# Last block of a three-block model: the scan's memory pool in two parts, the first chunk's decays and scores beside the convolution's norm

## The chip, the cores and the metric

One NeuronCore of a Trainium2 chip runs the whole program. The metric is the device time of one execution in microseconds (us); the time of a kernel is the median of its runs.

## What is computed

Three residual blocks run in series on 1024 tokens of width 1024, all in float32. The last one, which the change is mostly about, is this (cut):

```python
h = layer_norm(x, ln_emb_g, ln_emb_b)
proj = einsum('bld,de->ble', h, w_in)
xs, z, bm, cm, dt_raw, glu, cgate = split(proj, SPLITS, axis=-1)
xbc = silu(causal_depthwise_conv(concat([xs, bm, cm]), ssm_conv_w) + ssm_conv_b)
y = ssd_chunked(xh, dt, a, bm_c, cm_c) + d_skip * xh      # a scan over 8 chunks of 128 tokens, 2 groups
y_ssm = rms_norm_by_group(y * silu(z)) * ssm_norm_g
u = glu_a * sigmoid(glu_b)
u = causal_depthwise_conv(u, conf_conv_w) + conf_conv_b   # 31 taps
y_conf = silu(layer_norm(u, conf_ln_g, conf_ln_b)) * silu(cgate)
out = concat([y_ssm, y_conf]) @ w_out + b_out
h = layer_norm(alpha * h + out); h = layer_norm(alpha * h + sigmoid(h @ w_gate) * (p @ w_proj))
```

In a chunk the scan's output is `(C B^T * exp(segment sums)) @ xdt`, the diagonal part, plus `C @ state * exp(cumulative sum)`, the part that comes from the chunks before; the state is then decayed and raised by `B^T @ (xdt * decay)`. The second block, where the other part of the change lies, is an attention that keeps the top k keys of each query (called DSA here) and ends with a product with `od_w_out`.

## The kernel before

Each float32 product is made of three matmuls of 128x512 on split operands (lines 148 to 150, a "step" below): a weight is loaded as `wraw` on SP's queue, copied by ACT (`w`, L122), and its rest is taken by POOL (`w`, L123). `wraw` has 3 buffers, `w` has 13.

**Last block (`phase_c`).** DVE makes the 31-tap convolution channel by channel (`cy`, `cc`, L1323) and adds the channels up in `acc` (L1326). Meanwhile PE works through a list of filling steps: `filling` yields 128 steps for `cgate`, 128 for `z` and then 128 for the second half of `w_out`, on tiles `msC` that are made of the gated convolution output `cc`. PE's order in this place is written out by hand: `take(n)` issues the next n filling steps, `next(norm)` one part of `conf_norm`, and each turn of the loop over `ssd` one part of the scan. `conf_norm` makes the mean `mu` (PE, L1538), takes it off `cc` (DVE, L1544), squares (ACT) and sums (POOL), makes the variance `var` (PE, L1554), the factor `rb` (PE, L1560), multiplies (DVE, L1566) and ends with a silu on ACT (L1567). After that POOL multiplies `cc` by the gate `cgl` (L1395, 16 pieces, at most 4 for each turn of the scan), and only then can ACT and POOL make `msC` (L1358, L1359).

A chunk of `ssd` loads `xh`, `bct` and, for each of two groups, `ld`; DVE adds (L1698) and ACT takes Exp (L1700), which gives the decays; PE makes the scores `cb` (L1703, L1704); DVE multiplies (`cb` L1706, `ld` L1711); POOL makes `xd`, `xe` and scales `xh` (L1716 to L1723); for each group PE then makes `yoff`, `ydiag` and `inc`, and DVE and POOL add up `yS` and the state `st`. The tile sets of the scan lie in the pool `ssd`, which is opened after the pool `c_u` (the convolution's `acc`, `u` and the norm's `rsc`) is closed, and takes its memory. ACT, DVE, POOL and SP run their queues in order; a scheduler sets the order from the program, with PE's order given.

**Second block (`phase_b`).** POOL and ACT norm the query tiles (`hm`, `hr`, `qo`, then a store `d_q` from POOL's queue) while DVE finishes the top k. Then `DSA.front` loads a bias for each head as `lgB` on SP's queue and makes the softmax, unit by unit, and `out_tile` multiplies finished tiles by `od_w_out`. The first 8 weights of it are loaded only behind the bias loads of the second unit (`front_first`).

Of the kernel before, what the change touches and what calls it, by code (L numbers as in the profile page):

```python
# [11 lines left out]
F32 = mybir.dt.float32  # L12
# [7 lines left out]
P = 128  # L20
# [828 lines left out]
def phase_b(k, x, hout, hB):  # L849
# [64 lines left out]
    for b in range(2, 8):  # L914
        n = (b + 1) * P
# [78 lines left out]
    mix = mp.tile([P, 8, L], F32, name="mixB")  # L994
    with ExitStack() as c2:
        dp = c2.enter_context(k.pool("b_dsa"))
        wo = []
        ds = DSA(k, ep, dp, d_q, d_T, d_gate, kT, vB, sc, kg, mix)
        units = [(b, kv) for b in DORD for kv in range(2)]
        front = ds.front  # L1000

        def front_first(b, kv):
            front(b, kv)
            if (b, kv) == units[1]:
                with tc.issue_after(ds.bias_load.ins):
                    wo.extend(k.wchunk(Wo, 0, 512))
        ds.front = front_first
        pipeline(ds, units, lambda b: out_tile(k, mo, gp, b, 0, [mix], wo, x, hout, "sq", 1))
    sR.close()
    k.wdve = WDVE[3]  # L1010
# [149 lines left out]
class DSA:  # L1160
# [22 lines left out]
    def front(self, b, kv):  # L1183

        k, p, kT = self.k, self.p, self.kT
        with k.tc.high_priority(offset=2 * WPRIO if b == DORD[0] else 0):
            qT = self.load(b, kv)
        nc = k.nc
        V, S, G = nc.vector, nc.scalar, nc.gpsimd
        n = (b + 1) * P  # L1190
        st = p.tile([P, 5, 4], F32, tag="st", name="stB", bufs=3)
        hs, ts_ = slice(kv * 4, kv * 4 + 4), slice(b * P, (b + 1) * P)
        lgs = []
        for i in range(4):
            h = kv * 4 + i
            lg = (self.pe if i < 2 else p).tile([P, L], F32, tag="lg", name="lgB", bufs=4)
            lgs.append(lg)
            with k.tc.high_priority(offset=WPRIO):
                self.bias_load = nc.sync.dma_start(lg[:, :n], dap(self.d_T, h * P * 1152 + 127 + P * (7 - b), [[1151, P], [1, n]]))
            if b >= 2:  # L1200
                G.tensor_tensor(lg[:, :n], lg[:, :n], self.masks[b], op=ALU.add)  # L1201
            mx = -3e38
            for j, c0 in enumerate(range(0, n, 512)):
                w = min(512, n - c0)
                ps = k.ps("s")
                k.mm3(ps[:, :w], qT[:, 0, i], qT[:, 1, i], kT[:, 0, kv, c0:c0 + w], kT[:, 1, kv, c0:c0 + w],
                      True, True)
                V.tensor_tensor_reduce(lg[:, c0:c0 + w], ps[:, :w], lg[:, c0:c0 + w], 1.0, mx, ALU.add, ALU.max,
                                       st[:, 3 + j, i:i + 1])
                mx = st[:, 3 + j, i:i + 1]  # L1210
            V.tensor_scalar(st[:, 0, i:i + 1], mx, -1.0, None, op0=ALU.mult)
            S.activation(lg[:, :n], lg[:, :n], AF.Exp, bias=st[:, 0, i:i + 1], accum_out=st[:, 1, i:i + 1])
            V.reciprocal(st[:, 2, i:i + 1], st[:, 1, i:i + 1])
            S.activation(lg[:, :n], lg[:, :n], AF.Copy, scale=st[:, 2, i:i + 1])
        self.lgs[b, kv] = lgs
# [57 lines left out]
def phase_c(k, out, hC):  # L1273
# [18 lines left out]

    sF, (rp,) = stack(k.pool("c_conf"))
    cc = rp.tile([P, 8, L], F32, name="cc")
    sV, (up,) = stack(k.pool("c_u"))
    acc = up.tile([P, L], F32, name="acc")
    for j in range(4):
        w = [k.wpiece(W, kk, [(2576 + j * 256, 256), (3600 + j * 256, 256)]) for kk in range(KT)]
# [81 lines left out]
    with tc.manual_schedule(engines={mybir.EngineType.PE}):  # L1380
        take(128 + 58)
        norm = conf_norm(k, up, cc, acc, cw)
        for n in (43, 8, 0):
            next(norm)
            take(n)
        next(norm, None)
        sV.close()
        sS, (sp,) = stack(k.pool("ssd"))
        gated = 0
        for i, _ in enumerate(ssd(k, sp, steps, dtt, dtx, d_xs, d_bc, d_ys, d_cs)):  # L1390
            for _ in range(min(4, 16 - gated)):
                ct, cs = gated % 8, slice(gated // 8 * 512, gated // 8 * 512 + 512)
                cg = stage("cgl")
                nc.sync.dma_start(cg, d_cg[ct * P:(ct + 1) * P, cs])
                G.tensor_tensor(cc[:, ct, cs], cc[:, ct, cs], cg, op=ALU.mult)  # L1395
                gated += 1
            take(0 if i == 0 else 4 if i < 5 else 0 if i < 7 else 3)
        take(500)
    held.close()
    sS.close()  # L1400
# [265 lines left out]
    return tri, nacs, eac, dst, cdc  # L1666


def ssd(k, p, steps, dtt, dtx, d_xs, d_bc, d_ys, d_cs):
    nc, ins = k.nc, k.ins  # L1670
    V, S, G, T = nc.vector, nc.scalar, nc.gpsimd, nc.tensor
    f = lambda a: a.rearrange("p a b -> p (a b)")
    tri, nacs, eac, dst, cdc = steps
    first = {t: [p.tile([P, 512], F32, tag=t, name=n, bufs=2) for _ in range(2)]
             for t, n in (("y", "yS"), ("xe", "xe"), ("xd", "xd"))}

    def half(tag, name):
        return first[tag].pop(0) if first[tag] else p.tile([P, 512], F32, tag=tag, name=name, bufs=2)
    st = [p.tile([P, 512], F32, name=f"st{g}") for g in range(2)]
    for g in range(2):  # L1680
        V.memset(st[g], 0.0)
    b64 = lambda a, g, c: a[:, c, g * 8:g * 8 + 8].unsqueeze(2).to_broadcast([P, 8, 64])
    b64a = lambda a, c: a[:, c].unsqueeze(2).to_broadcast([P, 16, 64])
    h3 = lambda a: a.rearrange("p (h d) -> p h d", d=64)
    for c in range(8):
        ts_ = slice(c * P, (c + 1) * P)
        xhs = []
        for g in range(2):
            xhs.append(p.tile([P, 512], F32, tag="xh", name="xh", bufs=3))
            nc.sync.dma_start(xhs[g], d_xs[ts_, g * 512:(g + 1) * 512])  # L1690
        bct = p.tile([P, 4, P], F32, tag="bct", name="bct", bufs=2)
        nc.sync.dma_start(bct, d_bc[:, ts_].rearrange("(a n) t -> n a t", a=4))
        lds = []
        for g in range(2):
            ld = p.tile([P, 8, P], F32, tag="ld", name="ld", bufs=3)
            lds.append(ld)
            nc.sync.dma_start(ld, dap(d_cs, (c * 16 + g * 8) * P, [[0, P], [1, 8 * P]]))
            V._custom_dve(TENSOR_ADD_SAT, out=ld, in0=ld,  # L1698
                          in1=nacs[:, c, g * 8:g * 8 + 8].unsqueeze(2).to_broadcast([P, 8, P]), s0=0.0, s1=-3e38)
            S.activation(ld, ld, AF.Exp)  # L1700
        ps = k.ps("sd", "cb")
        for g in range(2):
            T.matmul(ps[:, g * P:(g + 1) * P], bct[:, g], bct[:, 2 + g], start=True, stop=True)  # L1703
            T.transpose(ps[:, 256 + g * P:256 + (g + 1) * P], bct[:, g], k.ident)  # L1704
        cb = p.tile([P, 2, P], F32, tag="cb", name="cb", bufs=1)
        V.tensor_tensor(cb, ps[:, :256].rearrange("p (g l) -> p g l", g=2),  # L1706
                        tri.unsqueeze(1).to_broadcast([P, 2, P]), op=ALU.mult)
        bt = p.tile([P, 2, P], F32, tag="bt", name="bt", bufs=1)
        S.activation(f(bt), ps[:, 256:512], AF.Copy)
        for g in range(2):  # L1710
            V.tensor_tensor(lds[g], lds[g], cb[:, g].unsqueeze(1).to_broadcast([P, 8, P]), op=ALU.mult)  # L1711
        yield
        xds, xes = [], []
        for g in range(2):
            xd = half("xd", "xd")
            G.tensor_tensor(h3(xd), h3(xhs[g]), b64(dtt, g, c), op=ALU.mult)  # L1716
            xds.append(xd)
        for g in range(2 if c < 7 else 0):
            xe = half("xe", "xe")
            G.tensor_tensor(h3(xe), h3(xds[g]), b64(dst, g, c), op=ALU.mult)  # L1720
            xes.append(xe)
        for g in range(2):
            G.tensor_tensor(h3(xhs[g]), h3(xhs[g]), dtx[:, 2, g * 8:g * 8 + 8].unsqueeze(2).to_broadcast([P, 8, 64]),  # L1723
                            op=ALU.mult)
        for g in range(2):
            gs = slice(g * 512, g * 512 + 512)
            po = k.ps("sd", "yoff")
            T.matmul(po, bct[:, 2 + g], st[g], start=True, stop=True)
            y = half("y", "yS")
            V.tensor_tensor(h3(y), h3(po), b64(eac, g, c), op=ALU.mult)  # L1730
            yield
            pd = k.ps("sd", "ydiag")
            for h in range(8):
                T.matmul(pd[:, h * 64:(h + 1) * 64], lds[g][:, h], xds[g][:, h * 64:(h + 1) * 64],  # L1734
                         start=True, stop=True)
            V.tensor_tensor(y, pd, y, op=ALU.add)
            G.tensor_tensor(y, y, xhs[g], op=ALU.add)
            nc.sync.dma_start(d_ys[ts_, gs], y)
            if c < 7:
                pi = k.ps("sd", "inc")  # L1740
                T.matmul(pi, bt[:, g], xes[g], start=True, stop=True)
                V.tensor_tensor(h3(st[g]), h3(st[g]), b64(cdc, g, c), op=ALU.mult)
                V.tensor_tensor(st[g], pi, st[g], op=ALU.add)
            yield
# [34 lines left out]
```

## Time and profile before

| | |
|---|---|
| median of 3 runs | 2072.5 us (2067.56, 2072.5, 2074.84) |
| the profiled execution's own time | 2079.29 us |
| its span, first to last instruction | 2077.6 us |
| TensorE (PE) busy | 1939.3 us, 93% |
| VectorE (DVE), ScalarE (ACT), GpSimd (POOL) busy | 1408.7, 922.2, 946.9 us |
| mean granted TensorE clock | 0.965 |

The profiled execution stands 6.8 us above the median of the runs. A timeline row gives start and length of a group of like instructions on one engine, and in brackets how long the engine stood idle before it and what released it. A row of the windows gives the busy time of each engine in a stretch.

### The profile page before, as it was taken

The page shows a single profiled execution, that of the slowest core. Times are in us where ns is not written, and L with a number is a line of the kernel's source. Part 1 is how long each engine was busy: PE and PEld are TensorE (multiplying, and loading weights), DVE is VectorE, ACT ScalarE, POOL GpSimd, SP SyncE. Part 2 cuts the span into 40 slices and gives each one's busy share as a digit, 9 for nine tenths or more (in the row PEclk, how much of TensorE's full clock was granted, in tenths as well). Part 3 has the DMA queues.
Part 4 walks back from the last instruction along what each step waited for, and adds up shares of the span by engine and source line. Part 5 has one row for each costly group of instructions (what it writes and reads, how often), then busy time and mean ns, then how long its engine had stood idle before and what let it go on. Part 6 is the DMA issues. An engine that isn't in the chain of part 4 may idle for free.

```text
span 2077.6 us, 27679 instructions
## 1 busy us (share of the span) xinstructions
PE 1939.3 (93%) x9291; PEld 1569.5 (76%) x9291; DVE 1408.7 (68%) x2847; ACT 922.2 (44%) x1831; POOL 946.9 (46%) x812
## 2 busy tenths in 40 slices
PE   7988989998999999799989999999999789999998
PEld 6767767777888877678767788788888657778786
DVE  8475513674559997677655399999998456657737
ACT  5222326664555897677756211245323431143210
POOL 5576415545422146765557221222223797545304
PEclk9998989999999999899999999999999889999999
DMA  6543342312322211563445232223333465474542
GB/s 202 152 123 101 109 147 84 112 44 92 99 64 77 67 42 57 176 215 136 132 160 182 88 101 68 71 93 92 112 105 109 147 207 187 142 253 157 178 147 102
DMA packets 166825, 256.20 MB, mean 123 GB/s; under 512 B 29207, under 2 KB 77677, under 8 KB 166683
## 3 DMA queue, kind: packets, MB, share of 16 engines
q1 hardware_dynamic: 155178, 232.43, 35.1%
q10 hardware_dynamic: 10224, 17.82, 2.3%
q0 software_dynamic: 1280, 4.20, 0.5%
q8 instruction: 73, 1.20, 0.2%
q14 instruction: 70, 0.57, 0.1%
HBM read 185.35 MB, written 75.06 MB: 125 GB/s over the span
## 4 chain that ended last, share of the span: by engine, by line
PE 59%; DVE 15%; DMA 9%; issue 6%; ACT 5%; POOL 5%; SPq 1%; DVEq 0%; POOLq 0%; ACTq 0%
PE mm L150 11%; PE mm L148 11%; PE mm L149 11%; DVE tkj L1114 2%; PE ydiag L1734 1%; PE pb L148 1%; PE pb L150 1%; PE pg L148 1%; PE pg L150 1%; PE pb L149 1%; PE pg L149 1%; PE pa L149 1%; PE pa L150 1%; PE pa L148 1%; POOL w L123 1%
## 5 line engine op out<-in xcount | busy, mean ns | idle before, releaser
L123 POOL TENSOR_TENSOR w<-wraw,w 128x512 fp32r<-128x512 f32 (+1 forms) x238 | 326.3, 1385 | 653.8 <-ACT w L122 647.2
L1323 DVE SCALAR_TENSOR_TENSOR cy<-u,cw,cy 128x1024 f32<-128x1024 f32 x232 | 298.6, 1287 | 5.7
L122 ACT ACTIVATE w<-wraw 128x512 fp32r<-128x512 f32 (+1 forms) x238 | 145.9, 623 | 186.2 <-DMA wraw<-in_w_in_dram 47.2
L148 PE MATMUL mm<-hnTC,w 128*128 128x512 f32 (+1 forms) x336 | 131.7, 392 | 0.0
L150 PE MATMUL mm<-hnTC,w 128*128 128x512 f32 (+1 forms) x336 | 131.6, 392 | 0.0
L149 PE MATMUL mm<-hnTC,w 128*128 128x512 f32 (+1 forms) x336 | 131.5, 391 | 0.0
L148 PE MATMUL mm<-w,ms 128*128 128x512 f32 x256 | 106.0, 414 | 9.0 <-ACT ms L1055 7.9
L1201 POOL TENSOR_TENSOR lgB<-lgB,sc 128x1024 f32<-128x1024 f32 (+5 forms) x48 | 81.1, 1724 | 67.1 <-DMA lgB<-d_T 65.5
L150 PE MATMUL mm<-w,ms 128*128 128x512 f32 x256 | 105.4, 413 | 4.5 <-POOL ms L1056 3.7
L1112 ACT ACTIVATE tkj<-sc,tks 128x896 bf16<-128x896 f32 (+2 forms) x93 | 96.7, 1041 | 22.1 <-DVE tks L1108 19.4
L149 PE MATMUL mm<-w,ms 128*128 128x512 f32 x256 | 104.0, 406 | 1.6 <-POOL w L123 1.6
L148 PE MATMUL mm<-w,hnTA 128*128 128x512 f32 (+1 forms) x192 | 72.6, 381 | 8.7 <-DVE qo L429 7.8
L148 PE MATMUL mm<-hnTB,w 128*128 128x512 f32 (+2 forms) x208 | 78.4, 377 | 0.2 <-DVE wit L886 0.2
L148 PE MATMUL mm<-w,hnTB 128*128 128x512 f32 x192 | 75.7, 395 | 2.9 <-ACT w L122 2.6
L149 PE MATMUL mm<-hnTB,w 128*128 128x512 f32 (+2 forms) x208 | 78.1, 376 | 0.0
L150 PE MATMUL mm<-hnTB,w 128*128 128x512 f32 (+2 forms) x208 | 78.1, 375 | 0.0
L149 PE MATMUL mm<-w,hnTB 128*128 128x512 f32 x192 | 74.7, 391 | 0.9 <-POOL w L123 0.9
L150 PE MATMUL mm<-w,hnTB 128*128 128x512 f32 x192 | 74.9, 390 | 0.0
L150 PE MATMUL mm<-w,hnTA 128*128 128x512 f32 (+1 forms) x192 | 72.8, 380 | 0.0
L149 PE MATMUL mm<-w,hnTA 128*128 128x512 f32 (+1 forms) x192 | 72.4, 378 | 0.3 <-POOL w L123 0.3
L148 PEld LDWEIGHTS mm<-hnTC,w 128*128 128x128 f32 (+1 forms) x336 | 61.6, 183 | 14.5
L149 PEld LDWEIGHTS mm<-hnTC,w 128*128 128x128 f32 (+1 forms) x336 | 61.6, 183 | 14.4
(612 smaller groups left out, 5896.0 us busy)
## 6 DMA issues: line engine op xcount, KB each, us to landing
wraw<-in_w_in_dram SPq DMA_DIRECT2D x56, 256.0 KB
wraw<-in_od_w_in_dram SPq DMA_DIRECT2D x48, 256.0 KB
wraw<-in_ev_w_in_dram SPq DMA_DIRECT2D x32, 256.0 KB
wraw<-in_w_in_dram SPq DMA_DIRECT2D x64, 128.0 KB
wraw<-in_w_out_dram SPq DMA_DIRECT2D x32, 256.0 KB
ld<-d_cs SPq DMA_DIRECT2D x16, 512.0 KB
hr<-h SPq DMA_DIRECT2D x24, 256.0 KB
d_T<-d_row SPq DMA_DIRECT2D x8, 576.0 KB
```

What stands on the lines that cost most here:

```text
L122: nc.scalar.activation(t[:, 0, :o], raw[:, :o], AF.Copy)
L123: nc.gpsimd.tensor_tensor(t[:, 1, :o], raw[:, :o], t[:, 0, :o].bitcast(F32), op=ALU.subtract)
L148: mm(out, aH, bH, start=start, stop=False)
L149: mm(out, aH, bL, start=False, stop=False)
L150: self.last = mm(out, aL, bH, start=False, stop=stop)
L1112: S.activation(self.junk(n), sc[b], AF.Sign, bias=cand[:, i:i + 1], accum_out=cnt[:, i:i + 1])
L1114: V.tensor_scalar(self.junk(n), sc[b], cand[:, i:i + 1], None, op0=ALU.is_ge, op1=ALU.add, accum_out=cnt[:, i:i + 1])
L1201: G.tensor_tensor(lg[:, :n], lg[:, :n], self.masks[b], op=ALU.add)
L1323: V.scalar_tensor_tensor(py if i < 30 else y, u[:, i:i + L], cw[:, ct, i:i + 1], py, op0=ALU.mult, op1=ALU.add)
L1734: T.matmul(pd[:, h * 64:(h + 1) * 64], lds[g][:, h], xds[g][:, h * 64:(h + 1) * 64], start=True, stop=True)
```

## The change

The pool `c_u` goes to the other side of memory, so that the scan's pool no longer has to wait for it. `ssd` is opened as soon as the norm is begun and holds what a chunk loads and computes up to the decayed scores; the rest (`st`, `xd`, `xe`, `yS`) lies in a second pool `ssd2`, opened by the callback `late` after `c_u` is closed. PE's hand-made order has the first chunk's `cb` 18 steps behind `mu`, 11 steps between `rb` and the end of the norm, and 3 where there were 4 between the scan's parts. In the second block the 8 weight loads of `od_w_out` are no longer held back.

```diff
 phase_b
-        wo = []
+        wo = k.wchunk(Wo, 0, 512)
         ds = DSA(k, ep, dp, d_q, d_T, d_gate, kT, vB, sc, kg, mix)
         units = [(b, kv) for b in DORD for kv in range(2)]
-        front = ds.front
-        def front_first(b, kv):
-            front(b, kv)
-            if (b, kv) == units[1]:
-                with tc.issue_after(ds.bias_load.ins):
-                    wo.extend(k.wchunk(Wo, 0, 512))
-        ds.front = front_first
 phase_c
-    sV, (up,) = stack(k.pool("c_u"))
+    sV, (up,) = stack(k.pool("c_u", side="right"))
...
         norm = conf_norm(k, up, cc, acc, cw)
-        for n in (43, 8, 0):
-            next(norm)
-            take(n)
+        sS, (sp,) = stack(k.pool("ssd"))
+        def late():
+            sV.close()
+            return sS.enter_context(k.pool("ssd2"))
+        scan = ssd(k, sp, late, steps, dtt, dtx, d_xs, d_bc, d_ys, d_cs)
+        next(norm)
+        take(18)
+        next(scan)
+        take(25)
+        next(norm)
+        take(7)
+        next(norm)
+        take(11)
         next(norm, None)
-        sV.close()
-        sS, (sp,) = stack(k.pool("ssd"))
         gated = 0
-        for i, _ in enumerate(ssd(k, sp, steps, dtt, dtx, d_xs, d_bc, d_ys, d_cs)):
+        for i, _ in enumerate(scan, 1):
...
-            take(0 if i == 0 else 4 if i < 5 else 0 if i < 7 else 3)
+            take(3 if i < 4 else 0 if i < 6 else 3)
 ssd
-    st = [p.tile([P, 512], F32, name=f"st{g}") for g in range(2)]
-    for g in range(2):
-        V.memset(st[g], 0.0)
...
         yield
+        if c == 0:
+            p2 = late()
+            st = [p2.tile([P, 512], F32, name=f"st{g}") for g in range(2)]
+            for g in range(2):
+                V.memset(st[g], 0.0)
-            xd = half("xd", "xd")
+            xd = p2.tile([P, 512], F32, tag="xd", name="xd", bufs=2)
```

(`xe` and `yS` likewise.) How the change moves instructions is shown at three places; line numbers of the changed kernel are 8 smaller up to the hand-made order and 1 or 6 smaller in `ssd`.

DVE in the changed kernel, in the sixth of the convolution's eight channels (`cy` and `cc` are the taps, `acc` the sum over channels):

```order
L1315 SCALAR_TENSOR_TENSOR cy<-u,cw,cy 128x1024 x15
L1692 ISA ld<-ld,nacs 128x1024
L1315 SCALAR_TENSOR_TENSOR cy<-u,cw,cy 128x1024
L1692 ISA ld<-ld,nacs 128x1024
L1315 SCALAR_TENSOR_TENSOR cc<-u,cw,cy 128x1024
L1692 ISA ld<-ld,nacs 128x1024
L1318 TENSOR_TENSOR acc<-acc,cc 128x1024
```

The three additions of decays (both groups of chunk 0, one of chunk 1) stood behind the whole norm before, after the product with `rb`; now they stand in the convolution, whose other taps are unchanged.

POOL in the kernel before, from the gates (`cc<-cc,cgl`) to the first `msC`:

```order
L1395 TENSOR_TENSOR cc<-cc,cgl 128x512 x9
L1716 TENSOR_TENSOR xd<-xh,dtt 128x512
L1395 TENSOR_TENSOR cc<-cc,cgl 128x512
L1737 TENSOR_TENSOR yS<-yS,xh 128x512
...
L1395 TENSOR_TENSOR cc<-cc,cgl 128x512 x4
L123 TENSOR_TENSOR w<-wraw,w 128x512
...
L123 TENSOR_TENSOR w<-wraw,w 128x512 x2
L1395 TENSOR_TENSOR cc<-cc,cgl 128x512
...
L1359 TENSOR_TENSOR msC<-cc,msC 128x1024 x2
```

and in the changed kernel:

```order
L1397 TENSOR_TENSOR cc<-cc,cgl 128x512 x6
L123 TENSOR_TENSOR w<-wraw,w 128x512 x2
...
L1715 TENSOR_TENSOR xd<-xh,dtt 128x512
L1736 TENSOR_TENSOR yS<-yS,xh 128x512
...
L1397 TENSOR_TENSOR cc<-cc,cgl 128x512 x2
L1719 TENSOR_TENSOR xe<-xd,dst 128x512
L1722 TENSOR_TENSOR xh<-xh,dtx 128x512
...
L1351 TENSOR_TENSOR msC<-cc,msC 128x1024 x2
```

From the first gate to `msC` POOL now has 11 gates, 5 `w`, 1 `xd`, 1 `xe`, 1 `xh` and 2 `yS`; before it had 16 gates, 4 `w`, 3 `xd`, 2 `xe`, 2 `xh` and 3 `yS`.

SP in the kernel before, at the start of the second block's softmax (`qf` is a normed query, `lgB` a bias):

```order
L110 DMA wraw<-in_od_w_in_dram 128x512 x34
L1173 DMA qf<-d_q 128x512
L1199 DMA lgB<-d_T 128x128 x4
L1173 DMA qf<-d_q 128x512
L1199 DMA lgB<-d_T 128x128 x4
L110 DMA wraw<-in_od_w_out_dram 128x512 x3
```

and in the changed kernel:

```order
L110 DMA wraw<-in_od_w_in_dram 128x512 x34
L110 DMA wraw<-in_od_w_out_dram 128x512 x8
L1165 DMA qf<-d_q 128x512
L1191 DMA lgB<-d_T 128x128 x4
L1165 DMA qf<-d_q 128x512
L110 DMA wraw<-in_od_w_out_dram 128x512 x2
L1191 DMA lgB<-d_T 128x128 x4
```

The eight loads moved ahead of the first query and the first biases; their copies on ACT and POOL moved with them, five into the head norms of the sixth and seventh tile of the first half, three into that of the last tile but one of the second half. Two loads of the next chunk of `od_w_out` now stand ahead of the biases of the first unit's third and fourth head.

## Rows read from the trace of the kernel before

**Rows 1.** The page: busy us of each engine, share of the span, instructions.
```profile
PE 1939.3 (93%) x9291; PEld 1569.5 (76%) x9291; DVE 1408.7 (68%) x2847; ACT 922.2 (44%) x1831; POOL 946.9 (46%) x812
```
**Rows 2.** Windows: busy us of PE, PEld, DVE, ACT, POOL; clock, DMA share, GB/s.
```profile
1620.00:1660.00 40.00, 26.99 (x124) 21.71 (x122) 22.80 (x27) 19.55 (x20) 29.75 (x19) 0.82 0.45 153
1660.00:1700.00 40.00, 31.02 (x120) 22.92 (x120) 18.92 (x18) 17.03 (x20) 40.00 (x28) 0.80 0.67 219
1700.00:1740.00 40.00, 38.85 (x189) 29.92 (x188) 28.81 (x29) 7.48 (x11) 31.68 (x24) 0.96 0.61 190
```
**Rows 3.** Timeline of PE, 1596 to 1695: norm, scan, first step on `msC`.
```profile
1596.88 1.88 PE L1538 MATMUL mu<-acc,ones 128*128 128x512 f32 x4
...
1635.70 1.95 PE L1560 MATMUL rb<-ident,rsc 128*128 128x128 f32 x16
1641.07 0.46 PE L1703 MATMUL cb<-bct 128*128 128x128 f32 x2 [3.42 <-DMA bct<-d_bc]
...
1647.20 2.05 PE L1728 MATMUL yoff<-st,bct 128*128 128x512 f32 x2 [5.23 <-DVE st L1681]
...
1657.55 3.65 PE L1734 MATMUL ydiag<-xd,ld 128*128 128x64 f32 x16 [4.07 <-DVE ld L1711]
...
1694.90 0.79 PE L150 MATMUL mm<-w,msC 128*128 128x512 f32 x1 [3.88 <-POOL msC L1359]
```
**Rows 4.** Timeline of DVE, 1589 to 1660.
```profile
1589.72 1.22 DVE L1326 TENSOR_TENSOR acc<-acc,cc 128x1024 f32<-128x1024 f32 x1
1597.94 9.66 DVE L1544 TENSOR_TENSOR cc<-cc,mu 128x512 f32<-128x512 f32 x16 [6.99 <-PE mu L1538]
...
1636.86 9.65 DVE L1566 TENSOR_TENSOR cc<-cc,rb 128x512 f32<-128x512 f32 x16 [6.37 <-PE rb L1560]
...
1647.51 1.55 DVE L1698 CUSTOM_DVE_ANT_1 ld<-ld,nacs 128x1024 f32<-128x1024 f32 x1
...
1655.12 4.50 DVE L1711 TENSOR_TENSOR ld<-ld,cb 128x1024 f32<-128x1024 f32 x2
```
**Rows 5.** Timeline of POOL, 1639 to 1697.
```profile
1641.48 1.04 POOL L1720 TENSOR_TENSOR xe<-xd,dst 128x512 f32<-128x512 f32 x1
...
1645.48 16.49 POOL L1395 TENSOR_TENSOR cc<-cc,cgl 128x512 f32<-128x512 f32 x9
...
1662.93 1.28 POOL L1395 TENSOR_TENSOR cc<-cc,cgl 128x512 f32<-128x512 f32 x1
...
1673.80 1.30 POOL L123 TENSOR_TENSOR w<-wraw,w 128x512 fp32r<-128x512 f32 x1
...
1677.28 2.25 POOL L1395 TENSOR_TENSOR cc<-cc,cgl 128x512 f32<-128x512 f32 x1
...
1692.50 4.67 POOL L1359 TENSOR_TENSOR msC<-cc,msC 128x1024 fp32r<-128x1024 f32 x2
```
**Rows 6.** Timeline of ACT: the norm's silu, a table load, an evacuation of `mm`.
```profile
1503.23 0.60 ACT L1339 ACTIVATE stg<-mm 128x512 f32<-128x512 f32 x1 [4.84 <-PE mm L150]
...
1642.37 9.17 ACT L1567 ACTIVATE cc<-cc,cw 128x1024 f32<-128x1024 f32 x8 [9.27 <-DVE cc L1566]
1651.55 1.28 ACT L1700 ACT_TABLE_LOAD   x1
1652.84 1.06 ACT L1700 ACTIVATE ld<-ld 128x1024 f32<-128x1024 f32 x1
```
**Rows 7.** Timeline of ACT in the second block: copies of `od_w_out`.
```profile
873.32 0.63 ACT L122 ACTIVATE w<-wraw 128x512 fp32r<-128x512 f32 x1 [2.43 <-DMA wraw<-in_od_w_out_dram]
...
883.78 0.63 ACT L122 ACTIVATE w<-wraw 128x512 fp32r<-128x512 f32 x1 [3.12 <-DMA wraw<-in_od_w_out_dram]
```
**Rows 8.** Timeline of POOL there: first head norm of the second half.
```profile
830.14 0.54 POOL L419 TENSOR_SCALAR hm<-hm 128x4 f32<-128x4 f32 x1 [5.04 <-ACT sq L418]
```

**Rows 9.** Windows of 5 us there, columns as in rows 2.
```profile
865.00:870.00 5.00, 3.95 (x19) 3.25 (x18) 2.52 (x17) 5.00 (x17) 3.72 (x3) 0.50 0.76 213
880.00:885.00 5.00, 4.90 (x27) 3.86 (x26) 1.40 (x10) 1.88 (x5) 2.13 (x3) 1.00 1.10 346
```

More of the change, by code (lines that the diff above doesn't have):

```diff
@@ L1198, in front @@
             with k.tc.high_priority(offset=WPRIO):
-                self.bias_load = nc.sync.dma_start(lg[:, :n], dap(self.d_T, h * P * 1152 + 127 + P * (7 - b), [[1151, P], [1, n]]))
+                nc.sync.dma_start(lg[:, :n], dap(self.d_T, h * P * 1152 + 127 + P * (7 - b), [[1151, P], [1, n]]))
             if b >= 2:
@@ L1666, in ssd_steps, with ssd @@
     return tri, nacs, eac, dst, cdc
-def ssd(k, p, steps, dtt, dtx, d_xs, d_bc, d_ys, d_cs):
+def ssd(k, p, late, steps, dtt, dtx, d_xs, d_bc, d_ys, d_cs):
     nc, ins = k.nc, k.ins
@@ L1673, in ssd @@
     tri, nacs, eac, dst, cdc = steps
[L1674 to L1678, printed above, removed]
-    st = [p.tile([P, 512], F32, name=f"st{g}") for g in range(2)]
-    for g in range(2):
-        V.memset(st[g], 0.0)
     b64 = lambda a, g, c: a[:, c, g * 8:g * 8 + 8].unsqueeze(2).to_broadcast([P, 8, 64])
@@ L1718, in ssd @@
         for g in range(2 if c < 7 else 0):
-            xe = half("xe", "xe")
+            xe = p2.tile([P, 512], F32, tag="xe", name="xe", bufs=2)
             G.tensor_tensor(h3(xe), h3(xds[g]), b64(dst, g, c), op=ALU.mult)
@@ L1728, in ssd @@
             T.matmul(po, bct[:, 2 + g], st[g], start=True, stop=True)
-            y = half("y", "yS")
+            y = p2.tile([P, 512], F32, tag="y", name="yS", bufs=2)
             V.tensor_tensor(h3(y), h3(po), b64(eac, g, c), op=ALU.mult)
```

## The prediction

> **What bounds the kernel now.** The page's busy times come first: PE is busy for 93% of the span, no other engine for more than 68% [rows 1]. So a gain must come from a place where PE stands still or runs at the lower clock. The windows show one: up to 1620 us each 40 us window of this block is full, then PE is busy for 27.0 and 31.0 us of 40 at a granted clock of 0.82 and 0.80, and from 1700 for 38.9 at 0.96 [rows 2]. That is where the convolution's norm hands over to the scan. While PE stands, POOL is busy for all 40.00 us of the second window [rows 2].
>
> PE's timeline says what it waits for, in order: the scores wait 3.42 us for their load, `yoff` 5.23 for the zeroed state, `ydiag` 4.07 for the decayed scores, and the first step on `msC` 3.88 for POOL's half of it, which lets PE go on at 1694.90 [rows 3]. The first three are the price of one thing: the scan's pool took the memory of the norm, so chunk 0's loads, decays and scores could only begin when `rb` was made (end at 1637.65, the start and length in [rows 3]). DVE shows it: it makes the product with `rb` until 1646.51, and only then decays (1.55 us each) and decayed scores (4.50 us for two) [rows 4]. The last wait is another: POOL must gate `cc` in 16 pieces, from 1645.48 on, before it makes `msC` at 1692.50 [rows 5].
>
> **Chunk 0 moved ahead.** The decays, `cb` and the two products with the scores go from behind the norm into DVE's and PE's waits. What they cost there:
>
> DVE gets three additions of 1.55 us [rows 4] in the convolution, 4.65 us. The sum `acc` ended at 1590.94 and `mu` ran at 1596.88, so DVE had 5.94 us to spare [rows 3, 4]. 1.29 us are left for waiting on the `ld` loads, which SP issues right before. No row shows that wait; a wait of chunk 0's kind was 3.42 us [rows 3], so `mu` is late by 0 to 2.1 us. I take **+0.5**, because the loads are issued some instructions before the addition.
>
> ACT gets three Exp among the silu evacuations of the filling steps. A load of the function table took 1.28 us, and the Exp began 1.29 us after it, 1.06 long [rows 6]. Two loads and an Exp make 3.6 us; ACT stood idle 4.84 us before such an evacuation [rows 6], so this hides, and costs nothing. If that cover were gone, PE would wait for its bank. The Trainium skill speaks against such mixing: ScalarE: Activation LUTs, What ACT_TABLE_LOAD costs, gives about 2.66 us for each switch, with a drain behind the load, and tells to do all functions of one set together. By that price an Exp with two switches would be 6.4 us, over the cover, and three of them would add some 4.6 us; the sum below would be -8. The trace disagrees on the drain: nothing stands between load and Exp here.
>
> The other products, 4.50 us and a small one, stand between DVE's subtraction, which ended at 1607.6, and the product at 1636.86 [rows 4]: 29 us with next to nothing in them. They cost nothing.
>
> **What PE then waits for.** From `rb` to the first `msC` step PE has the same filling (20 steps where there were 19), and no waits for chunk 0 but the one for the state's zeroing, which still stands behind DVE's product. So PE gets to the `msC` step by about 1660 to 1668, and there it stands: its order is fixed, and POOL decides. So the gain is what POOL gains.
>
> POOL before: gates from 1645.48, `msC` from 1692.50 [rows 5]. In the change `xd`, `xe` and `xh` of chunk 0 no longer stand between, since their data is there; the first gate waits for the first silu only, which took 9.17/8 = 1.15 us from 1642.37 on [rows 6]; with `rb` one step (0.7 us) earlier, the first gate is at 1642.8. Behind it come 11 gates, 5 `w`, 3 pieces for the chunk and 2 `yS`, as the order shows. Prices: a gate takes 1.28 us undisturbed, 16.49/9 = 1.83 beside DVE's decays, and up to 2.25 [rows 5]; `w` 1.30, a piece for a chunk 1.04 [rows 5], `yS` as a gate.
>
> - undisturbed: 11 x 1.28 + 5 x 1.30 + 3 x 1.04 + 2 x 1.28 = 26.3 us
> - at 1.83 for gates, `w` and `yS`: 18 x 1.83 + 3 x 1.04 = 36.1 us
>
> So `msC` begins between 1669 and 1679 and its first tile is there 4.67/2 = 2.3 us later, at 1671 to 1681, against 1694.90: 14 to 23 us earlier. PE owes 1.8 us at that point (`ydiag`, `inc` and `yoff` of chunk 1, which the fixed order now has behind it; estimated from the 16 small matmuls in 3.65 us at the low clock [rows 3]): **-12 to -21**.
>
> POOL owes more: 5 gates, 2 `xd`, `xe`, `xh` and a `yS`, less one `w`, some 10.6 to 13.3 us at the same prices. So it is where it stood at 1697.17 (end of `msC` [rows 5]) by 1684 to 1697: **0 to -13**, if POOL goes on being the bound. From 1700 on POOL is busy for 31.68 us of 40 and PE for 38.85 [rows 2], so POOL has some slack to catch up with and PE none. I take **-12**, between the two middles (-16 and -7), nearer to PE's.
>
> **Weights of the second block.** Removed from the start of the softmax: 8 loads, 8 ACT copies and the waits of 2.43 and 3.12 us that ACT has for two of them [rows 7]. PE is short of 1.05 us in one window and 0.10 in another, at a clock of 0.50 in the first, while DMA is at 1.10 of its engines in the second [rows 9]. So at most some 5.5 us come free, and PE shows 1 to 4 us for them to give.
>
> Added: five `w` of 1.30 us on POOL among the head norms, 6.5 us, of which a wait of 5.04 us behind them covers most [rows 8], and three, 3.9 us, in the last tile but one. The last tile's Exp stands behind ACT's own work, not behind these, so I count 1.5 of the first, and 1 for the biases of two heads, which now stand in SP's queue behind two loads that wait for those copies. Cost 1.5 to 5.4, taken as 2.5; gain 0 to 5.5, taken as 3.5: **-1**, range -4 to +5.
>
> **Sum.** +0.5 - 12 - 1 = -12.5 us. From the profiled execution's 2079.3 this is 2066.8; that execution stands 6.8 us above the median of the runs, so a median goes from 2072.5 to **2060.0 us**. About 0.3%, 6.2 us, is what a measurement of this kernel can tell from no change.
>
> **Rivals.**
> *PE is free after msC* (chance 0.17). POOL's debt never reaches PE: the windows' 31.68 of 40 speak for it, POOL's full 40.00 right before against [rows 2]. Then PE's range holds, with gates near 1.28 at -18, and with +0.5 and -1 that is 2054 us. GPSIMD Engine Reference, 1. Specifications, of the Trainium skill points the same way: POOL's interface to memory is shared with DVE and suffers from DVE instructions with two inputs there; by it the decays that left this stretch would let the gates run at their undisturbed length. The trace agrees in that a gate took 1.28 us at 1662.93, when DVE stood idle.
>
> *Nothing measurable* (0.23). POOL stays the bound with the longer prices (B about -4) and the second block's softmax begins later (+3): -0.5 with `mu`, 2072 us. For it: POOL is full in the windows that matter. Against it: the waits for the load and for the decayed scores have no reason any more.
>
> *POOL is slower than now* (0.12). In both places work for POOL is put beside more work of DVE. At 2.25 us, the worst row [rows 5], the stretch takes 18 x 2.25 + 3.1 = 43.6 us, `msC` starts at 1686.4, both its tiles end at 1691, and the debt of 5 x 2.25 + 4.2 brings POOL to 1706, 9 us behind. PE has then stood from 1665 to 1689 and gets the debt on top: +9; the five `w` of the second block, 11.3 us against the wait of 5.04, are +6 less 3.5 of gain: +11.5 in all, 2084 us. The point from which it decides: `msC` done later than about 1684, since then debt and start together pass 1697.
>
> **How the numbers follow.** The forecast has 0.48. Faster by over 0.3%: nearly all of it (0.45) and the first rival, 0.62. Within 0.3%: the second rival, the rest of the forecast's range and a little of the third, 0.27. Slower: 0.11. The range 2050 to 2073 takes in POOL's two bounds (-20 with the first rival) and the case of no change, and leaves out the third rival and a better end than -22.
>
> **What would show it.** Right: no wait of `cb` or `ydiag` for chunk 0; one long wait of PE, 8 to 15 us, before the first step on `msC`, ended by POOL at 1671 to 1681 (times against an unchanged first part); busy time of PE unchanged but for the clock; in the second block no ACT wait for `od_w_out` between 860 and 890. Wrong: `msC` after 1684; PE's waits for `w` or `xd` from POOL behind it, of 5 us and more; a wait of PE for a bank near 1505, or of DVE for `ld` there of over 3 us; Exp of the first unit later than 865.

## The result, and the profile after

The change made the kernel slower: a median of 2091.2 us (five runs, 2087.8 to 2094.7) against 2074.8 (five runs, 2067.6 to 2079.7) for the kernel before on the same chip. The two medians lie 16.4 us apart; the ratio estimated from all these runs is 1.0069 (95% interval 1.0049 to 1.0088), or +14.3 us (+10 to +18). The forecast was 12.5 us the other way, and the time lies outside its range. The profiled execution took 2088.5 us (span 2086.8).

The page's busy times answer to [rows 1]:

```profile
PE 1932.4 (93%) x9291; PEld 1564.1 (75%) x9291; DVE 1418.7 (68%) x2847; ACT 926.7 (44%) x1833; POOL 947.2 (45%) x812
```

PE is busy for 6.9 us less than before, and stands still for 16 us longer. Both programs issue the same 9291 matmuls. The start of the k-th matmul after, less that of the k-th before, says where time goes (only to some microseconds from 1641 to 1800, where filling and scan are mixed in another order):

| place (time in the kernel before) | after less before, us | lost or won since the row above |
|---|---|---|
| last unchanged stretch, 806 | -2.8 (differs from run to run) | |
| second block over, 1495 | +3.2 | +6.0 |
| convolution, 1540 | +5.4 | +2.2 |
| filling behind `rb`, 1658 | -8.9 | -14.3 |
| scan, 1738 | +0.7 | +9.6 |
| behind the scan, 1843 | -0.9 | -1.6 |
| output stage, 1859 | +7.7 | +8.6 |
| end | +9.3 | +1.6 |

So the change did win 14 us at the norm, and lost nearly twice as much elsewhere: 8.2 before it, 9.6 right behind it, and 8.6 at the end of the scan.

**The stretch it was meant for.** Timeline of PE after, its waits of 1 us and more from `rb` to 1720 (start, length, engine and line, operation, idle time before it and who ended that):

```profile
1654.49 1.10 PE L1727 MATMUL yoff<-st,bct 128*128 128x512 f32 x2 [2.04 <-DVE st L1711]
...
1672.90 0.50 PE L148 MATMUL mm<-w,msC 128*128 128x512 f32 x1 [3.39 <-ACT msC L1350]
...
1684.92 0.79 PE L150 MATMUL mm<-w,msC 128*128 128x512 f32 x1 [11.29 <-POOL msC L1351]
...
1699.33 1.12 PE L1740 MATMUL inc<-xe,bt 128*128 128x512 f32 x2 [1.50 <-POOL xe L1719]
...
1706.03 0.50 PE L149 MATMUL mm<-w,msC 128*128 128x512 f32 x1 [1.91 <-POOL w L123]
...
1708.23 0.50 PE L149 MATMUL mm<-w,msC 128*128 128x512 f32 x1 [1.24 <-POOL w L123]
```

The waits of chunk 0's `cb` and `ydiag` [rows 3] are gone, and in their place stand 14.7 us in front of `msC` (3.39 for ACT's half of it, 11.29 for POOL's). Against the 5.4 us by which this stretch starts late, the step at 1684.92 comes at 1679.5, where 1694.90 stood [rows 3]. POOL has no gap from 1660 on; one row of DVE stands with its own:

```profile
1650.98 5.01 POOL L1397 TENSOR_TENSOR cc<-cc,cgl 128x512 f32<-128x512 f32 x4 [6.39 <-ACT cc L1569]
...
1669.14 3.97 DVE L1705 TENSOR_TENSOR ld<-ld,cb 128x1024 f32<-128x1024 f32 x2
...
1669.77 4.48 POOL L1397 TENSOR_TENSOR cc<-cc,cgl 128x512 f32<-128x512 f32 x2
...
1682.53 4.66 POOL L1351 TENSOR_TENSOR msC<-cc,msC 128x1024 fp32r<-128x1024 f32 x2
...
1703.73 6.66 POOL L123 TENSOR_TENSOR w<-wraw,w 128x512 fp32r<-128x512 f32 x3
```

A gate takes 1.25 us in the first row of POOL and 2.24 in the second, which runs beside DVE's product of decays and scores. Windows after (columns as in [rows 2]):

```profile
1660.00:1700.00 40.00, 23.82 (x113) 17.85 (x111) 19.56 (x20) 15.31 (x20) 40.00 (x27) 0.83 0.68 239
1700.00:1740.00 40.00, 33.91 (x151) 24.94 (x150) 25.27 (x25) 6.01 (x8) 35.41 (x25) 0.91 0.46 152
...
1840.00:1860.00 20.00, 10.80 (x38) 8.42 (x37) 10.16 (x13) 10.68 (x22) 13.50 (x7) 0.66 0.76 278
```

From 1700 to 1740 PE is busy for 33.91 us where it was 38.85 [rows 2]: POOL's debt comes due as waits for `xe` (just before 1700) and `w`, 4.7 us in the three last rows of PE.

**The end of the scan.** Before the change PE waited 2.66 us here. First come rows of SP, POOL and PE of the kernel before (`smS` is a factor of the output norm, `tph` a transpose), then the same places after:

```profile
1814.95 7.17 SPq L1738 DMA_DIRECT2D d_ys<-yS  x2
...
1825.78 0.65 SPq L1426 DMA_DIRECT2D zO<-d_z  x1
...
1834.60 2.40 POOL L1428 TENSOR_TENSOR yO<-yO,zO 128x1024 f32<-128x1024 f32 x1 [9.22 <-DMA zO<-d_z]
...
1839.46 0.71 POOL L182 TENSOR_TENSOR smS<-smS,mhalf 128x2 f32<-128x2 f32 x1
...
1846.61 0.87 PE L195 MATMUL tph<-ident,yO 128*128 128x128 f32 x4 [2.66 <-DVE smS L1432]
```

```profile
1825.00 0.32 SPq L1737 DMA_DIRECT2D d_ys<-yS  x1
...
1828.58 1.01 SPq L110 DMA_DIRECT2D wraw<-in_w_out_dram  x2
...
1830.49 0.83 SPq L110 DMA_DIRECT2D wraw<-in_w_out_dram  x1
1831.36 0.65 SPq L1428 DMA_DIRECT2D zO<-d_z  x1
...
1840.64 2.38 POOL L1430 TENSOR_TENSOR yO<-yO,zO 128x1024 f32<-128x1024 f32 x1 [15.67 <-DMA zO<-d_z]
...
1845.30 2.33 POOL L1430 TENSOR_TENSOR yO<-yO,zO 128x1024 f32<-128x1024 f32 x1
1847.59 0.70 POOL L182 TENSOR_TENSOR smS<-smS,mhalf 128x2 f32<-128x2 f32 x1
...
1850.27 1.97 PE L195 MATMUL tph<-ident,yO 128*128 128x128 f32 x8 [7.63 <-ACT yO L1438]
```

The output stage's first tile hangs on a chain: the scan's last store, the loads that stand behind it in SP's queue, `yO` on POOL, `smS`, ACT's scaling of `yO`, and then the transposes. PE covers it with what is left of the `msC` steps. The change's numbers put 34 x 3 = 102 of the 128 steps into the scan where there were 32 x 3 = 96, so 26 are left instead of 32, 4.1 us less at 0.68 us each.

The chain itself is longer too. From the last store to ACT's scaling of the first tile it takes 24.5 us after (1825.00 to 1849.51) and 18.4 before (1821.80, the second store of the first row, to 1840.21). Two things moved in it: three weights now stand ahead of `zO` in SP's queue, and on POOL the second tile's `yO` stands ahead of the first `smS`.

The window 1840 to 1860 shows 10.80 us of PE where the kernel before had 17.34, and a granted clock of 0.66 where it had 0.91: after the wait the matmuls run at the lower level (1.2 GHz) up to about 1859.

**The second block.** Timeline of ACT in the last top-k steps (`tkj` a count of the top-k, `qo` the evacuation of a query tile), before and then after:

```profile
815.65 1.15 ACT L1112 ACTIVATE tkj<-sc,tks 128x1024 bf16<-128x1024 f32 x1 [0.78 <-DVE tks L1108]
...
817.37 0.60 ACT L415 ACTIVATE qo<-mm 128x512 f32<-128x512 f32 x1 [0.48 <-DMA d_q<-qo]
...
821.99 1.15 ACT L1112 ACTIVATE tkj<-sc,tks 128x1024 bf16<-128x1024 f32 x1 [2.63 <-DVE tks L1108]
...
826.94 1.15 ACT L1112 ACTIVATE tkj<-sc,tks 128x1024 bf16<-128x1024 f32 x1 [3.71 <-DVE tks L1108]
...
828.09 0.58 ACT L415 ACTIVATE qo<-mm 128x512 f32<-128x512 f32 x1
```

```profile
811.37 1.15 ACT L1104 ACTIVATE tkj<-sc,tks 128x1024 bf16<-128x1024 f32 x1 [0.28 <-DVE tks L1100]
...
816.41 0.63 ACT L122 ACTIVATE w<-wraw 128x512 fp32r<-128x512 f32 x1 [2.88 <-DMA wraw<-in_od_w_out_dram]
...
818.04 1.15 ACT L1104 ACTIVATE tkj<-sc,tks 128x1024 bf16<-128x1024 f32 x1 [1.00 <-DVE tks L1100]
...
820.23 0.60 ACT L415 ACTIVATE qo<-mm 128x512 f32<-128x512 f32 x1 [0.94 <-DMA d_q<-qo]
...
826.64 1.15 ACT L1104 ACTIVATE tkj<-sc,tks 128x1024 bf16<-128x1024 f32 x1 [4.44 <-DVE tks L1100]
...
831.73 1.15 ACT L1104 ACTIVATE tkj<-sc,tks 128x1024 bf16<-128x1024 f32 x1 [3.84 <-DVE tks L1100]
...
832.87 0.58 ACT L415 ACTIVATE qo<-mm 128x512 f32<-128x512 f32 x1
```

Five copies of `od_w_out` stand in ACT's queue here now (one is shown), and two `qo` come one count later: the first stood behind the count at 815.65 and now stands behind those at 811.37 and 818.04, the second follows two counts further on in both. The counts come at DVE's pace, 5 us a step. PE, whose banks these evacuations free, waits for them (waits of PE from 800 to 900, total, times, longest; after, then before):

```profile
PE mm L148 <- ACT qo L415: 8.3, 2, 6.9
```

```profile
PE mm L148 <- ACT qo L415: 0.3, 1, 0.3
```

### The profile page after: what moved, and what is told of

Read it like the earlier page. It is cut to its first block, busy times and chain, and to the rows that moved or that the text cites. A ratio compares the mean times of both kernels' runs of the same rounds, so it can differ in the third digit from the quotient of the medians.

```text
span 2086.8 us, 27675 instructions
## 1 busy us (share of the span) xinstructions
PE 1932.4 (93%) x9291; PEld 1564.1 (75%) x9291; DVE 1418.7 (68%) x2847; ACT 926.7 (44%) x1833; POOL 947.2 (45%) x812
## 4 chain that ended last, share of the span: by engine, by line
PE 46%; DVE 15%; issue 14%; DMA 10%; POOL 8%; ACT 6%; SPq 1%; DVEq 0%; POOLq 0%; ACTq 0%
PE mm L150 7%; PE mm L148 7%; PE mm L149 7%; POOL w L123 3%; DVE tkj L1106 2%; PE pb L148 1%; PE pb L150 1%; PE pb L149 1%; PE pa L149 1%; PE pa L148 1%; PE pa L150 1%; PE pg L149 1%; PE pg L148 1%; PE pg L150 1%; DMA wraw<-in_w_in_dram 1%
## 5 line engine op out<-in xcount | busy, mean ns | idle before, releaser
L148 PE MATMUL mm<-w,hnTB 128*128 128x512 f32 x192 | 77.5, 404 | 10.9 <-ACT qo L415 8.3
L148 PE MATMUL mm<-w,hnTA 128*128 128x512 f32 (+1 forms) x192 | 71.7, 377 | 9.1 <-DVE qo L429 9.1
L150 PE MATMUL mm<-w,hnTB 128*128 128x512 f32 x192 | 76.5, 399 | 0.0
L149 PE MATMUL mm<-w,hnTB 128*128 128x512 f32 x192 | 76.0, 398 | 0.4 <-POOL w L123 0.4
L148 PEld LDWEIGHTS mm<-hnTC,w 128*128 128x128 f32 (+1 forms) x336 | 61.6, 183 | 16.0 <-ACT stg L1331 1.6
L150 PEld LDWEIGHTS mm<-hnTC,w 128*128 128x128 f32 (+1 forms) x336 | 61.6, 183 | 15.4 <-POOL w L123 1.0
L149 PEld LDWEIGHTS mm<-hnTC,w 128*128 128x128 f32 (+1 forms) x336 | 61.6, 183 | 14.2
L149 PE MATMUL mm<-w,hnTA 128*128 128x512 f32 (+1 forms) x192 | 71.7, 374 | 0.4 <-POOL w L123 0.4
```

The costliest lines, as they stand in the source:

```text
L148: mm(out, aH, bH, start=start, stop=False)
L149: mm(out, aH, bL, start=False, stop=False)
L150: self.last = mm(out, aL, bH, start=False, stop=stop)
```

## The experiments

All ratios are to the kernel before, on the same chip; microseconds are made from them with its median there, 2081 to 2083 us. C stands for the scan's part of the change, A for the second block's.

**The two parts alone.** C is the change with this undone; A is the kernel before with this alone.

```diff
-        wo = []
+        wo = k.wchunk(Wo, 0, 512)
...
-                with tc.issue_after(ds.bias_load.ins):
-                    wo.extend(k.wchunk(Wo, 0, 512))
```

> The scan's part alone; the second block as in the kernel before. Theory (the loss has two halves): about 6 to 8 us slower than before, since the trace of the change loses 6 to 8 us in the second block and about as much net behind it (14 to 16 us won between the norm and the first msC step, 9 given back to GpSimd's debt by 1738 us, 8.6 at the end of the scan, 2 in the convolution). Rival 1 (the scan's part pays as forecast and all of the loss is the second block's): 10 to 13 us faster. Rival 2 (all of the loss is the scan's): 14 us slower. In the trace: the wait of tph for yO near the scan's end stays at about 7 us, and ScalarE's od_w_out waits are back at about 873 and 884 us.

> The second block's part alone; the last block as in the kernel before. Theory (two query evacuations come one top-k count later, so TensorE, GpSimd and the softmax start about 10 us late and win back 2 to 4): 6 to 8 us slower than before, with a TensorE wait of about 7 us for qo between 820 and 840. Rival 1 (as forecast): 0 to 2 us faster. Rival 2 (none of the loss is here, the offset in the changed trace is this run's own): no difference.

Measured: C alone 1.0045 (1.0026 to 1.0065), +9.4 us; A alone 1.0027 (1.0015 to 1.0039), +5.6 us. Both parts lose, and their sum, 15.0, is the change's 14.3 within the noise. C's loss is above the 6 to 8 us of the theory, but its interval, +5 to +14, takes them in. A's trace has the waits for `qo` again, 9.0 us in two.

**C with other places for the `msC` steps.** The first new line is the kernel with `msC` later, the second the tail cover.

```diff
-            take(3 if i < 4 else 0 if i < 6 else 3)
+            take(3 if i < 4 else 0 if i < 8 else 3)
+            take(3 if i < 4 else 0 if i < 6 else 3 if i < 34 else 2)
```

> The scan's part alone, but the first msC step stands two pieces of the scan later, at the place of the kernel before, so that 96 msC steps lie inside the scan and 32 behind it. Theory (TensorE waits 11 us for msC with work of the scan standing behind that wait, and 26 steps do not cover the output stage's first tile): 6 to 9 us faster than the scan's part alone, about level with the kernel before. Rival 1 (only GpSimd's sum of work counts, the order does not matter): within 2 us of the scan's part alone, with the wait moved to the pieces before msC. Rival 2 (the end of the scan alone counts): 4 us faster than the scan's part alone.

> The scan's part alone, msC where the change has it, but the scan's last six pieces take two msC steps each instead of three, so that 96 lie inside the scan and 32 behind it. Theory (the six steps are missing as cover for the chain from the last yS store to the first tph): the wait of tph for yO falls from 7.6 us to 2 to 4 and the time by 4 to 6 us against the scan's part alone. Rival 1 (the chain ends late because GpSimd or the loads are late, whatever stands before it): the wait stays above 6 us and the time within 1.5 us. Rival 2 (the thinner last pieces open waits inside the scan as large as those at its end): tph's wait falls, the time does not.

Measured: `msC` later 0.9996 (0.9985 to 1.0008), tail cover 0.9995 (0.9977 to 1.0013): each level with the kernel before and some 10 us below C alone. Six steps in other places undo the whole loss of C. Waits of PE behind the scan's end, in C alone, in tail cover, and in the change itself:

```profile
PE tph L195 <- DVE rS L1270: 7.0, 4, 2.7
PE tph L195 <- ACT yO L1446: 6.8, 1, 6.8
```

```profile
PE tph L195 <- DVE smS L1442: 3.5, 1, 3.5
```

```profile
PE tph L195 <- DVE rS L1262: 2.3, 1, 2.3
```

The wait of `tph` falls as expected. The time falls by some 10 us; the two intervals leave 5 to 16 for it, which takes in part of the 4 to 6 us that were expected. The 7.0 us for `rS` (the norm of the tiles behind the first) in C alone's trace explain nothing: the change has the same last block, and its trace shows 2.3.

What the six steps do is not their cover alone. Both kernels have the old order back: no weight ahead of `zO` on SP, the first `smS` ahead of the second `yO` on POOL, and the chain from the last store to ACT's scaling takes 18.5 and 18.6 us, against 23.7 in C alone. So in C alone the cover is 4 us shorter and the chain 5 us longer; no run has the one without the other, so what each costs in time stays open.

Starting `msC` later shortens POOL's wait for it from 12.2 to 7.2 us, but opens one of 13.5 for `xe`:

```profile
PE inc L1748 <- POOL xe L1727: 13.5, 2, 10.8
PE mm L150 <- POOL msC L1359: 7.2, 1, 7.2
```

So this order does not pay by itself; POOL has no less to do in it.

**Decays held, and `msC` on DVE.** Both start from the tail-cover kernel; a third takes both.

```diff
-            V._custom_dve(TENSOR_ADD_SAT, out=ld, in0=ld,
+            with k.tc.issue_after(k.cacc.ins):
+                V._custom_dve(TENSOR_ADD_SAT, out=ld, in0=ld,
...
-            G.tensor_tensor(m[:, 1], cc[:, :, ts_], m[:, 0].bitcast(F32), op=ALU.subtract)
+            (V if tt < 2 else G).tensor_tensor(m[:, 1], cc[:, :, ts_], m[:, 0].bitcast(F32), op=ALU.subtract)
```

> The scan's part with 96 msC steps inside (the tail-cover kernel), and the first decays of the scan (VectorE's three ld operations, and with them ScalarE's Exp) held behind the convolution's last sum. Theory (the table loads and Exp among the silu evacuations make TensorE wait for banks near 1510 and cost 2 us there): TensorE 40.00 of 40 us busy in 1500 to 1540, and 1 to 3 us faster than the tail-cover kernel. Rival 1 (the three ld operations, 1.2 us each, now stand ahead of the norm's subtractions on VectorE and cost what is won): within 1 us. Rival 2 (the stall is not ScalarE's): the waits for stg near 1510 stay.

> The tail-cover kernel, with the subtraction of the first two msC tiles on VectorE instead of GpSimd. Theory (GpSimd is the bound between the norm and 1700 us: gates, weights, xd, xe, xh and yS stand ahead of msC in its queue, and TensorE waits 12.2 us for it): the wait for msC falls to below 4 us, GpSimd's sum in the scan falls by 4.7 us, and the time falls by 5 to 10 us against the tail-cover kernel, 6 to 11 below the kernel before. Rival 1 (the gates, which msC needs in any case, are late): the wait stays above 8 us. Rival 2 (GpSimd's debt is due all the same, as waits for xd, xe or w): the wait moves and the time falls by less than 2 us.

> The tail-cover kernel with both edits: decays held behind the convolution, and the first two msC subtractions on VectorE. If the two theories hold and their gains add: 6 to 13 us faster than the tail-cover kernel, 7 to 14 below the kernel before. If only one of them holds: that one's gain alone. If both gains are waits that one and the same queue (GpSimd's) hands on: less than 3 us.

Measured: held 1.0006 (0.9987 to 1.0024), DVE 0.9971 (0.9958 to 0.9985), both 0.9995 (0.9981 to 1.0008). Holding the decays does clear the convolution. Windows of the change and of the kernel with the decays held:

```profile
1500.00:1540.00 40.00, 38.97 (x169) 31.07 (x168) 35.98 (x31) 19.57 (x24) 10.25 (x8) 1.00 0.58 182
```

```profile
1500.00:1540.00 40.00, 40.00 (x178) 33.12 (x177) 39.02 (x32) 9.03 (x15) 10.18 (x8) 1.00 0.56 178
```

But nothing is won: PE then waits 2.1 us for POOL's sum of squares (`acc`, in front of `var`) and 8.6 us for `w` from POOL, against 0.6 and 2.5 in the tail-cover kernel. That is the outcome of rival 1 by another way than its own, since `mu` was not late. `msC` on DVE wins 6 us against the kernel before. With both edits that gain is gone, so the two do not add. Waits of the kernel with `msC` on DVE, for the bank of the last z tile and for `msC`:

```profile
PE mm L148 <- ACT stg L1348: 7.5, 1, 7.5
PE mm L150 <- DVE msC L1359: 4.9, 1, 4.9
```

The wait of 12.2 us has become one of 4.9, and a new one of 7.5 stands behind it.

**What the second block pays for.** A alone, with the loads where the change has them and ACT's copies held behind its last work on the queries (evacuation and squares).

```diff
+                if behind is not None:
+                    with self.tc.issue_after(behind):
+                        nc.scalar.activation(t[:, 0, :o], raw[:, :o], AF.Copy)
...
+            k.hsq = S.activation(sq[:, hs], o[:, hs], AF.Square, accum_out=m[:, h:h + 1])
...
+        wo = [k.wpiece(Wo, kk, [(0, 512)], behind=k.hsq.ins) for kk in range(KT)]
```

> The second block's part alone, with the early od_w_out loads as the change has them, but ScalarE's copies of them held behind its last evacuation of the queries. Theory (the loads cost nothing, the copies cost because two evacuations slip behind one more top-k count): TensorE's waits for qo between 820 and 845 fall from 9 us to under 1 us, and the time is 0 to 2 us below the kernel before, 5 to 7 below the second block's part alone. Rival 1 (the early loads themselves, on SyncE's queue and the DMA engines ahead of the queries and biases, make the softmax late): still 4 to 8 us slower than before. Rival 2 (both): 2 to 4 slower.

Measured: 1.0016 (1.0001 to 1.0031), +3.3 us. The waits for `qo` are gone; at 842 us, where A alone is 11.3 us behind the kernel before, this one is 0.8. So the copies' place in ACT's queue makes those 10 us. The time is that of rival 2 (both cost something, 2 to 4 us slower), but its interval, 0 to 6 us, only just leaves out the theory (0 to 2 faster) and takes in A alone's +5.6. What the early loads cost by themselves is left open.

**Towards a version that beats both.** From the kernel with `msC` on DVE: the silu of the last z tile early; then, in addition, every second weight of `msC` on DVE.

```diff
-                S.activation(zt, ps, AF.Silu)
+                with tc.high_priority(offset=2 * WPRIO if ch and tt > 5 else 0):
+                    S.activation(zt, ps, AF.Silu)
...
+        yield
...
+            take(3 if i < 3 else 4 if i < 4 else 0 if i < 6 else 3 if i < 34 else 2)
...
+        k.wdve = 2
         w = [[k.wpiece(Wo, kk + 8, [(ch * 512, 512)], pool=op if ch * 8 + kk >= 13 else None, nx=3)
               for kk in range(8)] for ch in range(2)]
+        k.wdve = 0
```

> The kernel with the first two msC subtractions on VectorE, and the silu of the last z tile emitted right behind its last step instead of three pieces of the scan later, ahead of the weight copies in ScalarE's queue. Theory (in that kernel the bank of the last z tile is freed at 1694.6 us, behind weight copies that wait for their loads, though its sum is done near 1667, and TensorE stands 7.5 us for it): the wait for stg L1348 goes, and the time falls by 3 to 8 us against that kernel, 9 to 14 below the kernel before. Rival 1 (the next thing, GpSimd's weights, is as late): the wait turns into one for w of 5 us or more and the time falls by less than 2 us.

> As the kernel with the early z silu, and every second of the 16 weight pieces that msC multiplies is rounded and split on VectorE instead of ScalarE and GpSimd. Theory (GpSimd is still 40 of 40 us busy in 1660 to 1700, and eight of its weight operations there take 1.3 to 2.2 us each): the waits for w go, 2 to 6 us faster than the early-z-silu kernel. Rival 1 (VectorE works in order, and the weight copies wait for their loads with the scan's operations behind them): waits for ld or st take their place, no faster or up to 5 us slower.

Measured: early silu 0.9969 (0.9955 to 0.9983), no more than without it: the wait of 7.5 us is gone, and POOL's are there instead (rival 1):

```profile
PE mm L149 <- POOL w L123: 7.6, 3, 2.6
PE inc L1750 <- POOL xe L1729: 5.3, 1, 5.3
```

With half of the weights on DVE: 0.9942 (0.9927 to 0.9957), -12.1 us, the fastest of all. The waits for `w` and `xe` go but for 0.3 us, and waits for DVE come up in part (5.4 us for `msC`, 4.6 for decayed scores). PE's busy time in the stretch rises from 23.82 (the change) to 29.54, and DVE, which was idle for half of it, carries the work:

```profile
1660.00:1700.00 40.00, 29.54 (x125) 21.62 (x125) 36.52 (x32) 13.10 (x17) 39.06 (x25) 0.79 0.78 263
```

**The same edits without the change.** The kernel before with the `msC` line shown above, and with the two `wdve` lines too.

> The kernel before, with nothing but the first two msC subtractions on VectorE. Theory (there TensorE waits only 3.9 us for msC, and chunk 0's waits in front of it stay): 2 to 5 us faster than before, less than the same edit gains on the tail-cover kernel. Rival 1 (the whole gain of that edit has nothing to do with the scan's part): 6 us faster or more. Rival 2 (VectorE is the busier engine there): no faster.

> The kernel before, with the first two msC subtractions and every second weight piece of msC on VectorE, and nothing of the change. Theory (chunk 0 ahead of its time is worth something once GpSimd no longer holds up what comes behind it): 3 to 7 us faster than before, so 5 to 9 us slower than the same edits with the scan's part (0.9942 of before). Rival 1 (the whole gain of that kernel comes from GpSimd's relief, and chunk 0 ahead is worth nothing): 10 to 13 us faster. Rival 2 (the weights on VectorE gain nothing here, where TensorE waits in front of msC): 2 to 3 us faster, as with the msC subtractions alone.

Measured: 0.9986 (0.9973 to 0.9999), and with the weights 0.9999 (0.9983 to 1.0015). That is 2.9 us and nothing, where the two edits made 12 with the scan's part and the early silu. The 2.9 cannot be told from the 6 us of the first edit on the tail-cover kernel; with the weights too, -0.2 (-4 to +3) and -12.1 (-15 to -9) lie clear of each other. The early silu was not tried on the kernel before, where no wait for `stg` shows. Without chunk 0 ahead its waits stand in the way, and `msC`, now from DVE, is waited for as well. Waits of PE there, with the weights:

```profile
PE ydiag L1736 <- DVE ld L1713: 11.7, 5, 4.2
PE yoff L1730 <- DVE st L1683: 4.8, 1, 4.8
PE mm L150 <- DVE msC L1361: 4.7, 1, 4.7
PE cb L1705 <- DMA bct<-d_bc: 3.9, 1, 3.9
```

So chunk 0 ahead of its time is part of a gain of some 12 us, together with work taken off POOL and the old end of the scan; it does not pay by itself.

## Why the prediction was wrong

- **Second block, -1.** Failed in sign: +5.6 measured alone. I had counted the copies on POOL and the waits that ACT loses, but not the evacuations that stand behind the copies in ACT's queue. A copy of 0.63 us costs little there; what costs is the count that ACT then takes first, on DVE's beat. The sign named for a failure here is in the trace: the first unit's Exp, which was to come before 865, starts at 866.70 (862.17 before).
- **Chunk 0 ahead, +0.5.** `mu` was on time, as argued: DVE still idled 2.70 us before the product with it. ACT's Exp did make PE wait for banks between 1510 and 1540, where I had said they hide: +2.2, and with the decays held the stretch is full again. The cover was read from one evacuation's gap of 4.84 us; the three Exp, each with its loads of a table, came one behind the other (1509.00, 1513.65 and 1517.94) and did not all meet such a gap. By the Trainium skill's price (ScalarE: Activation LUTs, What ACT_TABLE_LOAD costs) the prediction's estimate was +4.6 us, which is too much here.
- **First step on `msC`.** Right: released at 1679.5 if the 5.4 us are taken off, inside 1671 to 1681 and 15.4 us earlier than before. The first gate came at 1645.6 with the same 5.4 us taken off, no earlier than before and 2.8 us later than the 1642.8 of the sum; the work from there to `msC` took 31.6 us, midway between its two bounds of 26.3 and 36.1.
- **POOL's debt.** This term was mis-sized: the two middles were -16 and -7, I took -12, and by 1738 9.6 of the 14.3 were given back; by 1843 the stretch stands at -6.3, the second middle. The window of 31.68 of 40 that was read as slack did not help, because the debt falls due in front of single steps of PE's fixed order (`xe`, `w`).
- **The end of the scan.** Not in the sum at all, and the largest error: +8.6 in the trace. The numbers of the diff say it (34 pieces of three steps instead of 32), and the prediction stopped at the first step on `msC` and never followed the filling to where it runs out. The tail-cover kernel, whose source differs from C alone in nothing but these six steps, is 10 us faster; the order that the scheduler makes behind the scan moves with them. Even so that kernel is only level with the one before (-1.0 us), where the sum without the second block was -11.5: the end of the scan is about half of the scan's error, the terms above are the rest.
- **Rivals.** "POOL is slower than now" had the sign and a time of 2084, by luck: its deciding point, `msC` later than 1684, was not reached. "PE is free after msC" read the gate at 1662.93 as one beside an idle DVE; in fact DVE ran 0.69 us from 1663.05. That a gate takes 1.25 us beside an idle DVE holds by a gate of the changed kernel, at 1688.16; but POOL did not get free.

The trace's items, +6.0 +2.2 -14.3 +9.6 -1.6 +8.6 +1.6, make +12.1; the comparison by time, +14.3 (+10 to +18).

## What to carry over

Work that fills waits is a fixed stock: when steps of it are pulled forward, look up what it covered where it now runs out, price that place too, and see whether loads change their order there. In an in-order queue a cheap instruction put early costs what the next one behind it then waits for, so list what it pushes past a slow beat. When one engine is full at a junction, taking work off it and taking away the waits in front belong together: here both made 12 us, work taken off POOL alone 3 at most, and the waits taken away alone nothing or a loss.

## What was not expected

Behind a wait of 12.24 us (tail-cover kernel, to 1682.80) a step's matmuls took 0.63 us up to about 1686, where they take 0.39 from 1689.65 on, and the granted clock of the window 1660 to 1700 there is 0.79, between its two levels (1.2 and 2.4 GHz): a wait cost more than its own length. And no wait ended alone: closing `msC`'s 12.2 us opened 7.5 for a bank, closing that opened 7.6 and 5.3 for POOL's `w` and `xe`, and only the third edit brought the time down further.
